# Dilated attention beside a projection: six-step attentions made into one stream of three-unit steps

## The chip, the core and the metric

The kernel runs on one core of a Trainium2 chip. The metric is the device time of one execution in microseconds, from the median of several runs. Engine names are those of the profile: PE is TensorE's matmul, PEld its weight load, DVE is VectorE, ACT is ScalarE, POOL is GpSimd, SP is SyncE, whose queue issues nearly all DMAs here.

## The reference

Two layers on a sequence of 1024 tokens of width 1024, in float32. Layer A is a gated MLP, layer B the attention that the change is about:

```python
for i in range(DEPTH):                       # DEPTH = 2
    h = rms_norm(x, norm_pre[i])
    y = gmlp_mixer(...) if i % 2 == 0 else dilated_attention_mixer(h, b_w_in, b_w_out, cos, sin)
    x = x + rms_norm(y, norm_post[i])

def dilated_attention_mixer(h, w_in, w_out, cos, sin):
    proj = h @ w_in                           # q, k, v of 3 groups x 16 heads x 64, and z
    for g, (window, dilation) in enumerate(((128, 1), (512, 4), (2048, 16))):
        q, k = apply_rope(...), apply_rope(...)
        o, lse = dilated_window_attention(q, k, qkv[:, :, g, 2], window, dilation)
    alpha = softmax(stack(lses), axis=0)      # weights of the three groups
    o = einsum('gbsh,gbshk->bshk', alpha, stack(outs))
    return (o * silu(z)) @ w_out
```

With 1024 tokens each group has eight blocks of 128 queries. A block of group 0 sees its own block and the one before it, in group 1 every second block does, and in group 2 a block sees only itself.

## The kernel before

Everything is written in a tile language whose scheduler sets the order of instructions on DVE, ACT, POOL and SP. The order on PE is that of the code in layer B (a manual schedule).

**The projection stream.** The product of `h` with the weights is cut into chunks: for each quarter `q` of the heads and each group `g` a chunk for V and two for Q and K (one for each pair of heads, `pr`), and now and then one for z. A chunk does seven products in a Strassen scheme, each float32 product as three matmuls on split operands (`mm3`, lines 83 to 85). In the profile these are `p_bv`, `p_bqk` and `p_bz`; below each is called a p. They follow each other without pause, and are the bulk of PE's work from about 790 us to 1825 us. The sums of products (`b_x`, `vt`) are made by ACT and DVE. The Q/K results are rotated on DVE and written to the tiles `Q` and `K` by 16 DMAs of a chunk (lines 703 and 704) on SP's queue.

**Attention between the p's.** `drive()` walks the stream three p's at a time (one yield). At a yield it adds `rate` to a credit, and when the credit is one it takes a step of the first generator in the queue `side`. With `RATE` = 0.16 a step comes every 18 or 21 p's. From chunk (3, 0, 1) on `RATE3` = 0.25 makes it 12. An attention, one of 24, (`attention(q, g, pr)`) becomes ready `WAIT` = 18 yields after its chunk's last product; it treats its eight blocks in four units of two, and has six steps:

```python
for s in range(6):
    if s >= 2: values(s - 2)      # po: V with PT       (line 796)
    if 1 <= s <= 4: transp(s - 1) # pT: St turned       (line 780)
    if s < 4: scores(s)           # s: Q with K         (line 755)
    yield
```

After `scores` DVE subtracts the maximum (line 764, two or four operations of a unit for each head), ACT takes the exponential into `St` (line 767); after `transp` ACT copies the result to `PT` (782); after `values` ACT copies to `oT` (801), and a DMA writes it to `od` (802). `turned()` transposes the V of both pairs (`pvt`, line 675, one step each) as soon as the V chunk is done. Every fourth yield `step_slow()` runs a piece of `merge`, which weighs the three groups' outputs of one pair of heads: it loads `mg`, `mo`, `mw`, multiplies on DVE, and turns the weights on PE (`wT`).

**Buffers.** The tiles `vt`, `Q` and `K` share a ring of five buffers (`qk_tile`). `St` has two buffers, `PT` one, `oT` two of 256 columns, `V` three, `st` (maxima and sums) one. PSUM has two banks for the scores, two for the transposes and one for `po`.

Of the kernel before, what the change touches and what calls it, by code (L numbers as in the profile page):

```python
# [15 lines left out]
P = 128  # L16
T = 1024
D = 1024
# [5 lines left out]
RATE = 0.16  # L24
WAIT = 18
# [3 lines left out]
RATE3 = 0.25  # L29
# [5 lines left out]
def trunk_kernel(  # L35
# [619 lines left out]
    def v_tile(n):  # L655
        return bp.tile([P, D], F32, tag="V", bufs=3, name=n)

    VS, QK, SZ = {}, {}, {}
    YL = {}

    def v_chunk(q, g):
        vts = {}

        def out(th, ct):
            if ct not in vts:
                vts[ct] = qk_tile(f"vt_{q}_{g}_{ct}")
            return vts[ct][:, th * 512:th * 512 + 512]

        def turned():
            for pr in range(2):  # L670
                V = v_tile(f"V_{q}_{g}_{pr}").rearrange("p (b h d) -> p b h d", b=8, h=2)
                for b4 in range(2):
                    pt = psum("t", [P, 4, P], f"pvt_{q}_{g}_{pr}_{b4}")
                    for j in range(4):
                        nc.tensor.transpose(out=pt[:, j, :], in_=toks(vts[pr], g, 4 * b4 + j, 1), identity=ident)
                    nc.scalar.copy(out=V[:, 4 * b4:4 * b4 + 4].rearrange("p j h d -> p j (h d)"), in_=pt)
                VS[q, g, pr] = V
                yield

        return proj_t(wb[q * 10 + g * 3], bops, newb, f"bv{q}{g}", lambda th, ct, o: None, out=out, done=lambda: later(turned(), 4))  # L680

    def qk_chunk(q, g, pr):
# [47 lines left out]
    merged = set()  # L730
    slow = deque()

    def attention(q, g, pr):


        nm = f"{q}_{g}_{pr}"
        Qt, Kt = QK[q, g, pr]
        S, PTs = {}, {}
        st = bp.tile([P, 8, 2, 2], F32, tag="st", bufs=1, name=f"st_{nm}")

        def prev_of(b):
            return (g == 0 and b > 0) or (g == 1 and b % 2 == 1)

        def scores(u):

            pss = [psum("s", [P, 2, 256], f"s_{nm}_{u}_{hh}") for hh in range(2)]
            for j in range(2):
                b = 2 * u + j
                prev = prev_of(b)
                o0 = 0 if prev else P  # L750
                for hh in range(2):
                    hs_ = slice(64 * hh, 64 * hh + 64)
                    q_ = block(Qt[hs_, :], g, b)
                    k_ = block(Kt[hs_, :], g, b, prev)
                    nc.tensor.matmul(out=pss[hh][:, j, o0:256].rearrange("p (n l) -> p n l", l=k_.shape[2]), lhsT=q_, rhs=k_, start=True, stop=True)  # L755
            for j in range(2):
                b = 2 * u + j
                o0 = 0 if prev_of(b) else P
                mk = mask[:, o0:256] if g < 2 else mask2
                St = bp.tile([P, 2, 256], F32, tag="St", bufs=2, name=f"St_{nm}_{u}_{j}")  # L760
                S[u, j] = St
                for hh in range(2):
                    with tc.high_priority(SOON):
                        nc.vector.tensor_tensor_reduce(  # L764
                            out=St[:, hh, o0:256], in0=pss[hh][:, j, o0:256], in1=mk, scale=-0.125, scalar=3.0e38,
                            op0=ALU.add, op1=ALU.min, accum_out=st[:, b, hh, 0:1])
                        nc.scalar.activation(  # L767
                            out=St[:, hh, o0:256], in_=St[:, hh, o0:256], func=AF.Exp, scale=-1.0,
                            bias=st[:, b, hh, 0:1], accum_out=st[:, b, hh, 1:2])

        def transp(u):

            PT = bp.tile([P, 2, 4, P], F32, tag="PT", bufs=1, name=f"PT_{nm}_{u}")
            PTs[u] = PT
            pT = [psum("t", [P, 4, P], f"pT_{nm}_{u}_{hh}") for hh in range(2)]
            use = [2 * j + kk for j in range(2) for kk in range(0 if prev_of(2 * u + j) else 1, 2)]
            sl = slice(1, 4, 2) if g == 2 else slice(use[0], 4)
            for hh in range(2):
                for k in use:
                    nc.tensor.transpose(out=pT[hh][:, k, :], in_=S[u, k // 2][:, hh, k % 2 * P:k % 2 * P + P], identity=ident)  # L780
                with tc.high_priority(SOON):
                    nc.scalar.copy(out=PT[:, hh, sl], in_=pT[hh][:, sl])

        def values(u):

            V, PT, b = VS[q, g, pr], PTs.pop(u), 2 * u
            po = psum("o", [P, 256], f"po_{nm}_{u}")
            if g == 2:
                todo = [(b, 1, 1, 0), (b + 1, 3, 1, P)]
            else:  # L790
                todo = [(b, 1, 2, 0), (b + 1, 3, 1, P)]
                if prev_of(b):
                    todo.insert(0, (b - 1, 0, 1, 0))
            for n, (kb, k, w, o) in enumerate(todo):
                for hh in range(2):
                    nc.tensor.matmul(  # L796
                        out=po[64 * hh:64 * hh + 64, o:o + w * P], lhsT=V[:, kb, hh, :], rhs=PT[:, hh, k:k + w, :].rearrange("p k i -> p (k i)"),
                        start=n == 0, stop=n == len(todo) - 1, skip_group_check=True)
# [3 lines left out]
            nc.sync.dma_start(out=od[q][pr][g][:, u * 256:u * 256 + 256], in_=oT)  # L802

        for s in range(6):
            if s >= 2:
                values(s - 2)
            if 1 <= s <= 4:
                transp(s - 1)
            if s < 4:
                scores(s)  # L810
            if s == 3:
                sv, ws = st.rearrange("p b h s -> p b (h s)"), slice(4 * g, 4 * g + 4)
                if g == 0:
                    nc.sync.dma_start(out=sd[q][pr].rearrange("(b i) w -> i b w", i=P)[:, :, ws], in_=sv)
                elif g == 1:
                    for n in range(2):
                        nc.sync.dma_start(
                            out=sd[q][pr].rearrange("(n i r) w -> n i r w", i=P, r=4)[n, :, :, ws],
                            in_=sv.rearrange("p (r n) w -> n p r w", n=2)[n])
                else:  # L820
                    nc.sync.dma_start(out=sd[q][pr].rearrange("(i b) w -> i b w", b=8)[:, :, ws], in_=sv)
            yield
        if g == 2 and q < 3:
            slow.append(merge(q, pr))

    def merge(q, pr, last=False):
# [15 lines left out]
        m = bp.tile([P, 8, 2], F32, tag="m", bufs=1, name=f"m_{nm}")  # L842
        e = bp.tile([P, 3, 2, 8], F32, tag="e", bufs=1, name=f"e_{nm}")
        nc.vector.tensor_tensor(out=m, in0=nmx[:, :, 0], in1=nmx[:, :, 1], op=ALU.min)
        nc.vector.tensor_tensor(out=m, in0=m, in1=nmx[:, :, 2], op=ALU.min)
        for g in range(3):
            sub(e[:, g].rearrange("p h b -> p b h"), m, nmx[:, :, g])
        nc.scalar.activation(out=e, in_=e, func=AF.Exp)
        for g in range(3):
            mul(sm[:, :, g], sm[:, :, g], e[:, g].rearrange("p h b -> p b h"))  # L850
        add(m, sm[:, :, 0], sm[:, :, 1])
        add(m, m, sm[:, :, 2])
        nc.vector.reciprocal(out=m, in_=m)
        for g in range(3):
            mul(e[:, g], e[:, g], m.rearrange("p b h -> p h b"))
# [7 lines left out]
        wT = bp.tile([P, 256], F32, tag="oT", bufs=2, name=f"wTs_{nm}")[0:48, 0:P]  # L863
# [24 lines left out]
        if last:  # L888
            if pr == 0:
                ws_ = [v_tile(f"mw_{nm}_0"), v_tile(f"mw_{nm}_1"), cos_t]  # L890
            else:
                ws_ = [sin_t, bp.tile([P, D], F32, tag="PT", bufs=1, name=f"mw_{nm}_1"), v_tile(f"mw_{nm}_2")]
            for g in range(3):
                for h in range(2):
                    nc.sync.dma_start(out=ws_[g][64 * h:64 * h + 64, :], in_=wd[q][pr][g, h].partition_broadcast(64))
            yield
            for th in range(2):
                ows = []
                for g in range(3):
                    wv_ = ws_[g][:, HALVES[th]].rearrange("p (i r) -> p i r", r=RUNS[g])  # L900
                    ov = os_[g].rearrange("p (r n i) -> p n r i", n=2, r=RUNS[g])[:, th] if g else os_[0][:, HALVES[th]].unsqueeze(1)
                    mul(wv_, ov.rearrange("p r i -> p i r"), wv_)
                    ows.append(ws_[g][:, HALVES[th]])
# [21 lines left out]
    credit, rate = [0.0], [RATE]  # L925
    now = [0]

    def later(gen, wait=0):
        side.append((now[0] + wait, gen))

    def step_side(force=False):
        while side:
            at, gen = side[0]
            if at > now[0] and not force:
                return False
            try:
                next(gen)
                return True
            except StopIteration:
                side.popleft()  # L940
        return False
# [66 lines left out]
    def fill():  # L1008
# [6 lines left out]
        for gen in busy:  # L1015
            run(gen)
# [7 lines left out]
    def attend():  # L1024
        m = merge(3, 0, True)
        for n, gen in enumerate(busy):
# [111 lines left out]
```

## Time and profile before

| | |
|---|---|
| median of three runs | 1942.67 us (1941.22 to 1943.18) |
| profiled execution | 1939.93 us, span 1938.2 us |
| mean granted PE clock | 0.989 |
| PE busy | 1860.0 us, 96% of the span |
| DVE, ACT, POOL busy | 67%, 52%, 26% |
| DMA | 125 GB/s on average |

PE is busy nearly all of the time, so the question for each instruction is whether it makes PE start its next matmul later, or takes PE's time itself. The times of the trace are microseconds from the start of the span.

### The profile page before, as it was taken

What the parts mean: (1) busy time and instruction counts of PE and PEld (TensorE: products, weight loads), DVE (VectorE), ACT (ScalarE), POOL (GpSimd) and SP (SyncE); (2) the same over time, 40 slices, a digit from 0 to 9 for tenths busy, and PEclk for the clock granted to TensorE, in tenths of its full rate; (3) what the DMA queues carried; (4) which work ended last, traced back from release to release, by engine and by line L of the source; (5) the groups of instructions that cost most, each with busy time, mean ns of one, the idle gap of its engine ahead of it and who ended that gap; (6) DMA issues with size and microseconds to landing.
All of it is one profiled execution on the core that took longest, in us unless ns stands there. A gap on an engine that the chain in (4) does not pass through costs nothing. (4 is left out here: it accounts for less than half of the span.)

```text
span 1938.2 us, 29972 instructions
## 1 busy us (share of the span) xinstructions
PE 1860.0 (96%) x10024; PEld 1492.9 (77%) x10024; DVE 1300.9 (67%) x2518; ACT 1016.1 (52%) x2332; POOL 499.9 (26%) x371
## 2 busy tenths in 40 slices
PE   6899999999999897999999999999999999999898
PEld 6899788888888676877777777777677776777677
DVE  7755866676455886658568783867665776867473
ACT  7544455555544564455545458455465446454831
POOL 4431334334200204212122222222123221122310
PEclk9999999999999998999999999999999999999999
DMA  5332434433267584223244543335542434433863
GB/s 207 99 119 90 140 113 138 122 105 106 77 202 232 173 256 135 81 74 89 72 94 108 158 112 108 79 75 148 147 110 83 99 93 138 123 77 80 228 200 111
DMA packets 233993, 242.25 MB, mean 125 GB/s; under 512 B 98672, under 2 KB 154608, under 8 KB 233840
## 3 DMA queue, kind: packets, MB, share of 16 engines
q1 hardware_dynamic: 233840, 240.34, 43.0%
q8 instruction: 80, 1.31, 0.3%
q14 instruction: 73, 0.60, 0.1%
HBM read 170.46 MB, written 44.63 MB: 111 GB/s over the span
## 5 line engine op out<-in xcount | busy, mean ns | idle before, releaser
L83 PE MATMUL p_bqk<-b_hi,whi_bqk 128*128 128x512 f32 x672 | 274.3, 408 | 1.2 <-DVE b_x_bqk L88 0.9
L85 PE MATMUL p_bqk<-b_hi,wlo_bqk 128*128 128x512 f32 x672 | 263.8, 393 | 0.0
L84 PE MATMUL p_bqk<-b_lo,whi_bqk 128*128 128x512 f32 x672 | 263.2, 392 | 0.0
L767 ACT ACTIVATE St<-St,st 128x128 f32<-128x128 f32 (+1 forms) x384 | 169.2, 443 | 173.6 <-DVE st L764 165.5
L83 PEld LDWEIGHTS p_bqk<-b_hi,whi_bqk 128*128 128x128 f32 x672 | 126.9, 189 | 40.4 <-issue 11.2
L85 PEld LDWEIGHTS p_bqk<-b_hi,wlo_bqk 128*128 128x128 f32 x672 | 126.7, 189 | 28.0
L84 PEld LDWEIGHTS p_bqk<-b_lo,whi_bqk 128*128 128x128 f32 x672 | 127.2, 189 | 23.6
L764 DVE CUSTOM_DVE_ANT_0 St<-s,mask 128x128 f32<-128x128 f32 (+1 forms) x384 | 111.7, 347 | 49.4 <-PE s L755 45.9
L83 PE MATMUL p_bv<-b_hi,whi_bv 128*128 128x512 f32 x336 | 137.6, 410 | 3.0 <-DVE vt L88 1.8
L85 PE MATMUL p_v<-whi_v,a_lo 128*128 128x256 f32 x448 | 128.3, 287 | 4.1 <-DVE sqa L368 2.3
L85 PE MATMUL p_bv<-b_hi,wlo_bv 128*128 128x512 f32 x336 | 131.6, 392 | 0.0
L84 PE MATMUL p_v<-wlo_v,a_hi 128*128 128x256 f32 x448 | 128.2, 287 | 3.5 <-DVE wlo_v L91 3.5
L84 PE MATMUL p_bv<-b_lo,whi_bv 128*128 128x512 f32 x336 | 131.4, 391 | 0.0
L83 PE MATMUL p_v<-whi_v,a_hi 128*128 128x256 f32 x448 | 128.3, 287 | 1.4 <-DVE v_s_v L88 0.8
L91 DVE TENSOR_TENSOR wlo_bqk<-wb_bqk,whi_bqk 128x512 fp32r<-128x512 f32 x96 | 81.4, 848 | 66.7 <-ACT whi_bqk L97 66.7
L91 POOL TENSOR_TENSOR wt_bqk<-wb_bqk,wt_bqk 128x512 f32<-128x512 f32 x48 | 71.7, 1494 | 202.4 <-DMA wb_bqk<-in_wb_dram 110.2
L85 PE MATMUL po<-oh,yl 128*128 128x512 f32 x256 | 100.6, 398 | 3.9 <-DVE yl L91 3.9
L84 PE MATMUL po<-ol,yh 128*128 128x512 f32 x256 | 100.6, 395 | 1.2 <-DVE ol L91 1.2
L83 PE MATMUL po<-oh,yh 128*128 128x512 f32 x256 | 101.3, 397 | 0.2 <-ACT yh L97 0.2
L97 ACT CAST whi_bqk<-wb_bqk 128x512 fp32r<-128x512 f32 x96 | 59.7, 622 | 71.5 <-PE p_bqk L84 44.1
L780 PE MATMUL pT<-ident,St 128*128 128x128 f32 x560 | 88.3, 285 | 7.9 <-ACT St L767 6.7
L91 POOL TENSOR_TENSOR wt_bqk<-wb_bqk,wb_bqk 128x512 f32<-128x512 f32 x24 | 32.8, 1365 | 234.8 <-DMA wb_bqk<-in_wb_dram 190.5
(260 smaller groups left out, 4854.0 us busy)
## 6 DMA issues: line engine op xcount, KB each, us to landing
wb_bqk<-in_wb_dram SPq DMA_DIRECT2D x96, 256.0 KB, 3.5
wr<-in_woa_dram SPq DMA_DIRECT2D x80, 256.0 KB, 3.5
yr<-yad SPq DMA_DIRECT2D x48, 256.0 KB, 3.3
wb_bv<-in_wb_dram SPq DMA_DIRECT2D x48, 256.0 KB, 3.2
Q<-b_c SPq DMA_DIRECT2D x192, 64.0 KB, 2.1
K<-b_c SPq DMA_DIRECT2D x192, 64.0 KB, 2.0
od<-oT SPq DMA_DIRECT2D x96, 128.0 KB, 2.6
mo<-od SPq DMA_DIRECT2D x36, 256.0 KB, 3.4
```

Source lines behind the costliest of these rows:

```text
L83: nc.tensor.matmul(out=pso, lhsT=l_hi, rhs=r_hi, start=start, stop=False, skip_group_check=chained)
L84: nc.tensor.matmul(out=pso, lhsT=l_hi, rhs=r_lo, start=False, stop=False, skip_group_check=chained)
L85: nc.tensor.matmul(out=pso, lhsT=l_lo, rhs=r_hi, start=False, stop=stop, skip_group_check=chained)
L91: (eng or nc.vector).tensor_tensor(out=out, in0=a, in1=b, op=ALU.subtract)
L97: nc.scalar.copy(out=hi, in_=src)
L764: nc.vector.tensor_tensor_reduce(out=St[:, hh, o0:256], in0=pss[hh][:, j, o0:256], in1=mk, scale=-0.125, scalar=3.0e38, op0=ALU.add, op1=A ...
L767: nc.scalar.activation(out=St[:, hh, o0:256], in_=St[:, hh, o0:256], func=AF.Exp, scale=-1.0, bias=st[:, b, hh, 0:1], accum_out=st[:, b, h ...
L780: nc.tensor.transpose(out=pT[hh][:, k, :], in_=S[u, k // 2][:, hh, k % 2 * P:k % 2 * P + P], identity=ident)
```

## The change

The six-step generators are replaced by objects `Unit`. A queue of units runs through all attentions; `attend(unit)` does one step with three units in a row: the transposes of the last unit, the values of the one before it, and the scores of the new one. A unit of groups 0 and 1 has two blocks as before, one of group 2 has four. The V of the second pair of heads is turned after the first two units of the first pair's attention. The rates are lower, the wait shorter, and buffers are dealt out anew: `V` 2, `st` 2, `PT` 2, `oT` one of 512 columns, `St` a tile for each head. The end is rewritten to fit (`ending`), and the last merge uses other tiles.

```diff
-RATE = 0.16
-WAIT = 18
+RATE = 0.125
+WAIT = 16
...
-RATE3 = 0.25
+RATE3 = 0.16
...
-        return bp.tile([P, D], F32, tag="V", bufs=3, name=n)
+        return bp.tile([P, D], F32, tag="V", bufs=2, name=n)
...
+        def done():
+            TURN[q, g] = turned(1)
+            later(turned(0), 4)
...
-            later(attention(q, g, pr), WAIT)
-            if (q, g, pr) == (3, 0, 1):
+            later(lambda: attention(q, g, pr), WAIT)
+            if (q, g, pr) == (3, 2, 1):
                 rate[0] = RATE3
...
+        def __init__(self, att, u):
+            self.q, self.g, self.pr, self.st = att
+            self.n = 4 if self.g == 2 else 2
+            self.b, self.last = self.n * u, self.n * u + self.n == 8
...
+            self.S = [bp.tile([P, 512], F32, tag="St", bufs=2, name=f"St_{self.nm}_{hh}") for hh in range(2)]
...
-            PT = bp.tile([P, 2, 4, P], F32, tag="PT", bufs=1, name=f"PT_{nm}_{u}")
+            self.PT = bp.tile([P, 2, 4, P], F32, tag="PT", bufs=2, name=f"PT_{self.nm}")
...
-            oT = bp.tile([P, 256], F32, tag="oT", bufs=2, name=f"oT_{nm}_{u}")
+            oT = bp.tile([P, 512], F32, tag="oT", bufs=1, name=f"oT_{self.nm}")[:, 0:w]
...
+    def attention(q, g, pr):
+        st = bp.tile([P, 8, 2, 2], F32, tag="st", bufs=2, name=f"st_{q}_{g}_{pr}")
+        units = [Unit((q, g, pr, st), u) for u in range(2 if g == 2 else 4)]
+
+        return units[:2] + [TURN.pop((q, g))] + units[2:] if pr == 0 else units
+
+    going = [None, None]
+
+    def attend(unit):
+
+        if going[0]:
+            going[0].transp()
+        if going[1]:
+            going[1].values()
+        if unit:
+            unit.scores()
+        going[:] = [unit, going[0]]
...
-    credit, rate = [0.0], [RATE]
+    credit, rate = [0.5], [RATE]
```

In the whole program the attentions now break into the p stream 114 times and not 175: 78 steps of transposes, values and scores, four partial ones, 24 of V and 8 of `wT`. The matmuls are the same in number. The copies to `PT` go from 192 to 160, those to `oT`, and their DMAs, from 96 to 80.

Two places show how instructions move; names are tile_q_g_pr_unit, and a row ends with the shape of the result. The first is PE in attention (1, 2, 0), third group. Before, a middle step stands thus between two p's:

```order
L85 MATMUL p10_bv20_12369<-b_hi2_5165,wlo2_bv20_12229 128x512
L796 MATMUL po_1_2_0_0_12373<-PT_1_2_0_0_12305,V_1_2_0_12044 64x128 x4
L780 MATMUL pT_1_2_0_1_0_12382<-ident_69,St_1_2_0_1_0_12320 128x128
L780 MATMUL pT_1_2_0_1_0_12382<-ident_69,St_1_2_0_1_1_12325 128x128
L780 MATMUL pT_1_2_0_1_1_12383<-ident_69,St_1_2_0_1_0_12320 128x128
L780 MATMUL pT_1_2_0_1_1_12383<-ident_69,St_1_2_0_1_1_12325 128x128
L755 MATMUL s_1_2_0_2_0_12390<-K_1_2_0_12062,Q_1_2_0_12061 128x128
L755 MATMUL s_1_2_0_2_1_12391<-K_1_2_0_12062,Q_1_2_0_12061 128x128
```

The matching step of the changed kernel, of which the last p ahead and the first scores are shown (eight rows of scores follow each other, then a p):

```order
L85 MATMUL p00_bqk2_0_0_12400<-b_hi1_5163,wlo1_bqk2_0_0_12341 128x512
L799 MATMUL pT_1_2_0_1_0_12415<-ident_69,St_1_2_0_1_0_12229 128x128 x4
L799 MATMUL pT_1_2_0_1_1_12416<-ident_69,St_1_2_0_1_1_12230 128x128 x4
L815 MATMUL po_1_2_0_0_12427<-PT_1_2_0_0_12198,V_1_2_0_11866 64x128 x8
L766 MATMUL s_1_2_1_0_0_12439<-K_1_2_1_12253,Q_1_2_1_12252 128x128
L766 MATMUL s_1_2_1_0_1_12440<-K_1_2_1_12253,Q_1_2_1_12252 128x128
```

The values now stand between transposes and scores, and a step holds twice as many of each. The second place is PE at the end of the scores of attention (0, 1, 0), before:

```order
L755 MATMUL s_0_1_0_3_0_8960<-K_0_1_0_8512,Q_0_1_0_8511 128x128
L755 MATMUL s_0_1_0_3_1_8961<-K_0_1_0_8512,Q_0_1_0_8511 128x128
L755 MATMUL s_0_1_0_3_0_8960<-K_0_1_0_8512,Q_0_1_0_8511 128x256
L755 MATMUL s_0_1_0_3_1_8961<-K_0_1_0_8512,Q_0_1_0_8511 128x256
L83 MATMUL p00_bv02_8709<-b_hi7_5175,whi7_bv02_8818 128x512
L84 MATMUL p00_bv02_8709<-b_lo7_5176,whi7_bv02_8818 128x512
```

And after, where `p20` is a partial product of V chunk (0, 2), one of its seven:

```order
L799 MATMUL pT_0_1_0_2_0_8990<-ident_69,St_0_1_0_2_0_8940 128x128 x3
L799 MATMUL pT_0_1_0_2_1_8991<-ident_69,St_0_1_0_2_1_8941 128x128 x3
L815 MATMUL po_0_1_0_1_9000<-PT_0_1_0_1_8915,V_0_1_0_8584 64x256 x2
L815 MATMUL po_0_1_0_1_9000<-PT_0_1_0_1_8915,V_0_1_0_8584 64x128 x2
L766 MATMUL s_0_1_0_3_0_9008<-K_0_1_0_8512,Q_0_1_0_8511 128x128
L766 MATMUL s_0_1_0_3_1_9009<-K_0_1_0_8512,Q_0_1_0_8511 128x128
L766 MATMUL s_0_1_0_3_0_9008<-K_0_1_0_8512,Q_0_1_0_8511 128x256
L766 MATMUL s_0_1_0_3_1_9009<-K_0_1_0_8512,Q_0_1_0_8511 128x256
L83 MATMUL p20_bv02_8886<-b_hi3_5167,whi3_bv02_8899 128x512
L84 MATMUL p20_bv02_8886<-b_lo3_5168,whi3_bv02_8899 128x512
L85 MATMUL p20_bv02_8886<-b_hi3_5167,wlo3_bv02_8900 128x512
```

On DVE the changed kernel has, right behind the four reductions of this unit's scores, the two sums into `vt`, of which the first reads `p20` before the p's shown may add to it; the `ISA` rows are the reductions of line 774 and the reads of their results:

```order
L774 ISA St_0_1_0_3_0_9014,st_0_1_0_8676<-s_0_1_0_3_0_9008,mask_7392 128x128
L774 ISA st_0_1_0_8676 128x1
L774 ISA St_0_1_0_3_0_9014,st_0_1_0_8676<-s_0_1_0_3_0_9008,mask_7392 128x256
L774 ISA st_0_1_0_8676 128x1
L774 ISA St_0_1_0_3_1_9015,st_0_1_0_8676<-s_0_1_0_3_1_9009,mask_7392 128x128
L774 ISA st_0_1_0_8676 128x1
L774 ISA St_0_1_0_3_1_9015,st_0_1_0_8676<-s_0_1_0_3_1_9009,mask_7392 128x256
L774 ISA st_0_1_0_8676 128x1
L88 TENSOR_TENSOR vt_0_2_1_8952<-p20_bv02_8886,b_x2_0_bv02_8950 128x512
L88 TENSOR_TENSOR vt_0_2_1_8952<-p20_bv02_8886,b_x1_0_bv02_8848 128x512
```

`vt_0_2_1` takes over the ring buffer of this attention's `Q`, so its first sum can't stand ahead of the last scores. Before, 33 p's and another attention step lay between those scores and the p of `p20` that waits for the sum; now there is none.

## Rows read from the trace of the kernel before

**Rows 1.** Page, part 1: busy us (share of the span) and instructions, by engine

```profile
PE 1860.0 (96%) x10024; PEld 1492.9 (77%) x10024; DVE 1300.9 (67%) x2518; ACT 1016.1 (52%) x2332; POOL 499.9 (26%) x371
```

**Rows 2.** PE's waits, 790 to 1665 us: total us, times, longest

```profile
PE pT L780 <- ACT St L767: 5.8, 7, 2.1
PE po L796 <- ACT oT L801: 3.5, 3, 1.7
PE p_bv L83 <- DVE vt L88: 1.8, 1, 1.8
```

**Rows 3.** PE's waits, 1665 to 1825 us

```profile
PE s L755 <- issue: 2.4, 3, 2.0
```

**Rows 4.** Windows: length, busy us of each engine, PE clock, DMA share, GB/s

```profile
790.00:1665.00 875.00, 861.98 (x4746) 659.61 (x4745) 605.62 (x1345) 471.85 (x1293) 202.74 (x136) 1.00 0.41 106
1665.00:1686.00 21.00, 17.58 (x76) 13.57 (x75) 20.47 (x23) 4.49 (x8) 5.89 (x4) 0.96 0.42 108
1686.00:1691.00 5.00, 5.00 (x15) 3.48 (x12) 4.07 (x12) 1.73 (x8) 0.02 (x1) 0.50 0.23 78
...
1765.00:1825.00 60.00, 56.58 (x327) 41.30 (x326) 35.15 (x101) 42.15 (x119) 18.47 (x11) 1.00 0.64 163
```

**Rows 5.** Timeline of PE, scores alone: start, us, line, operation, count

```profile
981.93 0.39 PE L84 MATMUL p_bqk<-b_lo,whi_bqk 128*128 128x512 f32 x1
982.16 0.39 PE L85 MATMUL p_bqk<-b_hi,wlo_bqk 128*128 128x512 f32 x1
982.48 0.71 PE L755 MATMUL s<-K,Q 64*128 64x128 f32 x8
...
983.46 0.39 PE L84 MATMUL p_bqk<-b_lo,whi_bqk 128*128 128x512 f32 x1
```

**Rows 6.** Timeline of PE, a full step of group 2

```profile
1292.07 0.39 PE L85 MATMUL p_bqk<-b_hi,wlo_bqk 128*128 128x512 f32 x1
1292.39 0.66 PE L796 MATMUL po<-PT,V 128*64 128x128 f32 x8
1292.98 0.66 PE L780 MATMUL pT<-ident,St 128*128 128x128 f32 x4
1293.57 0.71 PE L755 MATMUL s<-K,Q 64*128 64x128 f32 x8
...
1294.55 0.39 PE L84 MATMUL p_bqk<-b_lo,whi_bqk 128*128 128x512 f32 x1
```

**Rows 7.** Timeline of PE, eight transposes of V

```profile
1050.51 0.39 PE L85 MATMUL p_bv<-b_hi,wlo_bv 128*128 128x512 f32 x1
1050.75 1.03 PE L675 MATMUL pvt<-ident,vt 128*128 128x128 f32 x8
...
1051.85 0.40 PE L84 MATMUL p_bv<-b_lo,whi_bv 128*128 128x512 f32 x1
```

**Rows 8.** DVE, timeline 1087 us, and reductions by form: busy us, mean ns

```profile
1087.10 0.68 DVE L88 TENSOR_TENSOR vt<-p_bv,b_x_bv 128x512 f32<-128x512 f32 x1
L764 DVE CUSTOM_DVE_ANT_0 St<-s,mask 128x256 f32<-128x256 f32 x176 | 68.3, 419 | 10.6 <-PE s L755 10.6
```

**Rows 9.** PE and SP, timeline, last product of chunk (2, 2, 0) and last K

```profile
1502.31 0.39 PE L85 MATMUL p_bqk<-b_hi,wlo_bqk 128*128 128x512 f32 x1
1514.35 0.61 SPq L704 DMA_DIRECT2D K<-b_c  x1
```

**Rows 10.** Page, part 6: queue, count, KB of one, us to landing

```profile
K<-b_c SPq DMA_DIRECT2D x192, 64.0 KB, 2.0
od<-oT SPq DMA_DIRECT2D x96, 128.0 KB, 2.6
```

**Rows 11.** ACT's waits ahead of line 801, and one of them in its timeline

```profile
1625.70 0.37 ACT L801 COPY oT<-po 128x256 f32<-128x256 f32 x1 [2.29 <-DMA od<-oT]
ACT oT L801 <- DMA od<-oT: 10.8, 4, 3.5
```

More of the change, by code (lines that the diff above doesn't have):

```diff
@@ L728, in z_chunk, with prev, scores @@
         return proj_t(wb[q * 10 + 9], bops, newb, f"bz{q}", z_out, hooks={2: lambda: prep(0), 7: lambda: prep(1)} if q == 3 else None)
-    merged = set()
+    merged, through = set(), set()
     slow = deque()
[L733 to L750, printed above, removed]
+    class Unit:
+        def __init__(self, att, u):
+            self.q, self.g, self.pr, self.st = att
+            self.n = 4 if self.g == 2 else 2
+            self.b, self.last = self.n * u, self.n * u + self.n == 8
+            self.nm = f"{self.q}_{self.g}_{self.pr}_{u}"
+            self.lone = self.g == 2
+            if self.lone:
+                self.use = [[j] for j in range(4)]
+            else:
+                self.use = [[2 * j + kk for kk in range(0 if self.prev(self.b + j) else 1, 2)] for j in range(2)]
+            self.first = self.use[0][0]
+        def prev(self, b):
+            return (self.g == 0 and b > 0) or (self.g == 1 and b % 2 == 1)
+        def scores(self):
+            Qt, Kt = QK[self.q, self.g, self.pr]
+            pss = [psum("s", [P, 512], f"s_{self.nm}_{hh}") for hh in range(2)]
+            for j, use in enumerate(self.use):
+                b, cs = self.b + j, slice(use[0] * P, use[-1] * P + P)
@@ L781, in transp @@
                 with tc.high_priority(SOON):
[L782 to L789, printed above, removed]
-            else:
[L791 to L794, printed above, removed]
+                    nc.scalar.copy(out=self.PT[:, hh, self.first:], in_=pT[hh][:, self.first:])
@@ L795, in values @@
+        def values(self):
+            V, w = VS[self.q, self.g, self.pr], self.n * P
+            po = psum("o", [P, w], f"po_{self.nm}")
+            if self.lone:
+                todo = [(self.b + j, j, 1, j * P) for j in range(4)]
+            else:
+                todo = [(self.b, 1, 2, 0), (self.b + 1, 3, 1, P)]
+                if self.first == 0:
+                    todo.insert(0, (self.b - 1, 0, 1, 0))
+            for n, (kb, k, m, o) in enumerate(todo):
                 for hh in range(2):
@@ L924, in trunk_kernel, with later @@
     side = deque()
-    credit, rate = [0.0], [RATE]
+    credit, rate = [0.5], [RATE]
     now = [0]
-    def later(gen, wait=0):
-        side.append((now[0] + wait, gen))
+    def later(work, wait=0):
+        side.append((now[0] + wait, work))
     def step_side(force=False):
         while side:
-            at, gen = side[0]
+            at, work = side[0]
             if at > now[0] and not force:
                 return False
+            if isinstance(work, Unit):
+                side.popleft()
+                attend(work)
+                return True
+            if callable(work):
+                side.popleft()
+                side.extendleft((at, w) for w in reversed(work()))
+                continue
             try:
-                next(gen)
+                next(work)
                 return True
@@ L940, in step_side @@
                 side.popleft()
+        if (force or rate[0] != RATE) and any(going):
+            attend(None)
+            return True
         return False
@@ L1014, in fill @@
                 yield
-        for gen in busy:
-            run(gen)
+        while step_side(True):
+            pass
         for c in (6, 7):
@@ L1022, in fill, with ending @@
                 yield
-    def attend():
+    def ending():
         m = merge(3, 0, True)
-        for n, gen in enumerate(busy):
-            for _ in gen:
-                if n == len(busy) - 1:
-                    next(m, None)
-                yield
+        while step_side(True):
+            if (3, 2, 0) in through:
+                next(m, None)
+            yield
         yield from m
         yield from merge(3, 1, True)
-    busy = [gen for _, gen in side]
-    side.clear()
-    rest = attend()
+    rest = ending()
     for n, _ in enumerate(fill()):
```

149 lines of the change are left out of this document (73 added, 76 removed).

## The prediction

> **What bounds the kernel.** I read the page first: PE is busy 1860.0 us, 96% [rows 1]. The change touches layer B alone, so windows come next. From 790 to 1665 us PE is busy 861.98 of 875 us at full clock, and DVE and ACT have 605.62 and 471.85 [rows 4]: PE's own work is the bound there, with 13.0 us lost. From 1665 to 1686 us 3.4 us are lost, behind that five microseconds run at clock 0.50 (2.5 us lost), and from 1765 to 1825 us 3.4 us are lost, all by the same rows. That makes 22.3 us. The reader is to see two things to win: these 22 us, and PE's work itself. PE's waits name the first: transposes for the exponentials (5.8 us in 7 waits), values for the copy to `oT` (3.5 in 3), a p of V for the sum into `vt` (1.8 in 1) [rows 2], and later scores that wait for K (2.4; longest 2.0) [rows 3]. A change of some microseconds on PE is therefore a change of the whole; idle time of other engines costs nothing.
>
> **What a step costs PE.** Consecutive p's start 0.227 us apart (0.23 in the first two of [rows 5], which are rounded to 0.01). The cost of an interruption is the time from the p ahead to the second p behind, less two such intervals.
> - Scores alone: 983.46 - 982.16 - 0.454 = 0.846 [rows 5].
> - Values, transposes and scores of one unit of group 2: 1294.55 - 1292.07 - 0.454 = 2.026 [rows 6].
> - Eight transposes of V: 1051.85 - 1050.51 - 0.454 = 0.886, or 0.111 each [rows 7].
>
> Transposes use the array as p's do (128*128 in the rows), and take twice what their 128 columns would at 0.227 for 512. Scores and values use it otherwise (64*128 and 128*64), two heads beside each other. Eight such rows are four pairs, so by the transposes' pitch 4 x 0.11 = 0.44. What is left of 0.846 is 0.41 for two borders (p to scores, scores to p), 0.20 each. The full step has four borders (p, values, transposes, scores, p) and 2.026 - 3 x 0.44 = 0.70 left, 0.175 each. So each time PE goes over between unlike uses it loses 0.17 to 0.20 us, and a transposition next to a p loses nothing.
>
> Now count borders. Before, an attention has 2 + 2 + 4 + 4 + 2 + 2 = 16 in its six steps, 24 times: 384. After, a step is transposes, values, scores: p to transposes is free, three borders are left. 78 steps and 8 borders in the partial ones make 242. Two things are in this: the order within a step, and the third group, whose 32 units of each kind have 16 groups where 32 stood. The difference is 142 x 0.175 = **-25 us**. No row shows values directly ahead of scores. From below: if that border cost nothing, 78 more go, -38. From above: if it cost as much as leaving for a p and coming back, two, 78 are added, and 64 x 0.175 = -11. I take one border, because values to transposes and transposes to scores are single borders in [rows 6] and fit the same price.
>
> The Trainium skill bears on this, "TensorEngine Tiling (Array Packing)", section Key Properties under Tiling Modes: going from one tiling mode to another drains TensorE, while other tiles of the same mode don't. By that rule values to scores is one drain like any other, and the term is the -25 above; by a price for the distance between the uses it would be the -11. The trace agrees as far as it goes: four borders of 0.175 and two of 0.20.
>
> **Waits that go.** Steps are now 24 p's apart, 5.4 us and the step itself, where they were 18 (4.1 us), and 18 (16 at the end) instead of 12 in the dense stretch. The distance from scores to their transposes becomes 24, that from transposes to values at least 18, where values stood as few as 12 p's behind their transposes or directly behind the last `oT` copy. I take the waits on `oT` and `wT`, the one on `vt` at 1087 us, and one of the seven long ones on the exponentials as gone: 3.5 + 1.8 + 1.0, with their starts about 7 of the 13.0 us. The other 6 stay: there DVE itself is held by `merge`, which waits for DMAs, and a longer distance gives only 0.3 us more, since before the values (about 1.0 us) stood ahead of the transposes. The scores' wait near 1684 us, with the low clock behind it, was 5.9 us; it goes from this place. The dense stretch, 3.4 us, goes. Sum **-16.3**.
>
> **Waits that come.**
> - `vt`: in four V chunks, (0, 2), (1, 1), (2, 1), (3, 1), a p now follows scores directly and needs a sum that stands on DVE behind four reductions. Two pairs of reductions (one of 0.419 [rows 8]; the shorter ones 0.29) and the sum of 0.68 [rows 8] are 2.1 us after the first scores' end, of which the rest of the scores covers some 0.8: 1.3 each, **+5.2** (bounds +4 and +9, the latter with another DVE operation ahead). Behind the waiting p stands all of PE.
> - Q and K: the last product of chunk (2, 2, 0) starts at 1502.31 and ends 0.39 later; its last K is issued at 1514.35 [rows 9] and lands 2.0 later [rows 10], 13.65 us after. The first scores came 66 p's on and did not wait. With the shorter `WAIT` and the coarser steps they come after 48 p's at (0, 0, 0), (1, 2, 0) and (2, 2, 0): 10.9 us and 1.7 of transposes and values, 12.6 at most. That is 1.1 each, and in four other chunks where other steps lie between, about 1 each: **+7.6** (bounds +3.6 and +12, if each late one also brings a stretch at clock 0.50 as in [rows 4]).
> - `oT`: one buffer, so ACT's copy waits for the DMA of the copy before. Landing takes 2.6 us from issue [rows 10], a step is 8.0 us, so only a DMA held on SP's queue is late. **+2.5**, one such place; above, see the rivals.
>
> Fewer copies on ACT, the smaller `merge`, and `V` with two buffers lie beside PE's stream: DVE and ACT have 269 and 403 us idle in the 875 [rows 4]. Were ACT the bound, 48 copies fewer of 0.37 us [rows 11] would be worth 18 us more. The matmuls of the end are the same, and I take nothing there.
>
> Sum: -25 - 16.3 + 15.3 = **-26.0**, from the profiled 1939.93 to about 1914. The median of the runs was 2.7 us above that execution; I forecast **1915 us**.
>
> **Rivals.**
> 1. *Values to scores cost two borders.* For it: the two uses differ in both sides of the array. Against: nothing in the rows charges a border by what lies on its two sides. Then -11 instead of -25: 1929 us.
> 2. *The new waits don't come*, since the whole stream shifts and with it what DMAs and DVE meet: the four `vt` sums find DVE free, Q and K land in time. For it: Q and K had landed at 66 p's without a wait, and their delay is SP's issue time of 0.6 us each, which other orders shorten. Against: the distance 0 of the `vt` sums is fixed by the order. 1915 - 13 = 1902 us.
> 3. *The single `oT` decides, and the kernel is slower.* SP issues in order; the 16 DMAs of Q and K take 0.61 each [rows 9], so a DMA of `oT` behind all of them lands 9.8 + 2.6 = 12.4 us after its copy, against 8.0 until the next copy. ACT then stands 4.4 us, with the exponentials of the new scores queued behind it; the transposes have 1.3 us of slack, so PE loses up to 3.1. Before, two buffers gave twice the time, and still ACT waited 10.8 us in 4 places, in one of them 2.29 with PE behind it [rows 11]. In SP's new order 17 of 80 of these DMAs have 12 or more Q and K issues since the one before. All 17 at full price are 53 us in place of the 2.5: 1965 us. From nine on the gain is gone, from 11 the kernel is slower (1915 - 2.5 + 34 = 1947). Against: 96 copies waited in 4 places [rows 11], so most of these DMAs are issued before such a queue builds up. The Trainium skill, "Trainium Kernel Development and Optimization", section Best Practices, advises two buffers for what is moved by DMA; here the trace shows waits even with two.
> 4. *PE's work is less, but another bound takes it:* weights for the p's, prepared by POOL, ACT and DVE, come late. Against: no wait of a p on weights in [rows 2, 3]. With half of the 25 lost, 1928 us.
>
> **Chances.** Forecast 0.55 (1904 to 1925 for itself), rival 1 0.17, rival 2 0.13, rival 3 0.10, rival 4 0.05. About 0.2%, 3.9 us, is what a measurement can tell from no change. Only rival 3 reaches above 1939, and not in all of its cases; with what the others leave open: faster 0.88, same 0.05, slower 0.07. Range 1898 to 1938: below it lies the free border together with rival 2, above it rival 3 in earnest.
>
> **What would show it.** In the changed profile: a full step of group 2 (eight transposes, sixteen values, sixteen scores) between two p's costing 3 x 0.88 + 3 x 0.18 = 3.2 us; 3.5 would speak for rival 1. PE's busy time falling by some 20 us with the same matmuls. Waits of `p_bv` on `vt` at four places; waits of scores on K or `issue` at the starts of attentions; no waits of `po` on `oT` of more than a few microseconds in sum, and ACT's on `oT` DMAs below about 15. The forecast is wrong if ACT stands for `oT` in nine places or more, or if PE's busy time stays.

## The result and the profile after

| | before | changed |
|---|---|---|
| median | 1941.95 us (1938.92 to 1943.18, 4 runs) | 1913.93 us (1912.29 to 1919.63, 4 runs) |
| ratio, 95% interval | | 0.9863 (0.9839 to 0.9888) |
| profiled execution, span | 1938.2 us | 1913.5 us |

The kernel is 1.4% faster; 1915 us had been forecast. The page of the changed kernel, part 1, to set beside [rows 1]:

```profile
PE 1834.7 (96%) x10024; PEld 1507.0 (79%) x10024; DVE 1310.4 (68%) x2518; ACT 1002.7 (52%) x2280; POOL 503.6 (26%) x371
```

The same 10024 matmuls take PE 25.3 us less, and the span is 24.7 us shorter. Nearly all of it is one stretch. First the window of the kernel before from 790 us to its last values, then that of the changed kernel (length, busy time of each engine, clock, DMA share):

```profile
790.00:1825.00 1035.00, 1015.14 (x5566) 774.22 (x5565) 713.29 (x1581) 560.72 (x1540) 241.76 (x160) 1.00 0.41 107
```

```profile
790.00:1801.00 1011.00, 987.22 (x5563) 786.08 (x5562) 717.54 (x1582) 548.25 (x1487) 246.15 (x160) 0.99 0.42 108
```

Almost the same matmuls lie in both. The stretch is 24.0 us shorter: busy time falls by 27.9 us, idle time rises from 19.9 to 23.8. So the gain is PE's work, and the waits are a little worse. Busy time holds some time at a low clock too: taken in windows of 1 us, PE's busy time times what the clock lacked to 1.00 is an estimated 4.9 us in the stretch before and 6.8 in that of the changed kernel. Without it PE's work fell by some 30 us. A full step of the third group, timeline of PE:

```profile
1267.28 0.39 PE L85 MATMUL p_bqk<-b_hi,wlo_bqk 128*128 128x512 f32 x1
1267.51 1.03 PE L799 MATMUL pT<-ident,St 128*128 128x128 f32 x8
1268.47 1.09 PE L815 MATMUL po<-PT,V 128*64 128x128 f32 x16
1269.50 1.16 PE L766 MATMUL s<-K,Q 64*128 64x128 f32 x16
...
1270.93 0.40 PE L84 MATMUL p_bv<-b_lo,whi_bv 128*128 128x512 f32 x1
```

It costs 1270.93 - 1267.28 - 0.454 = 3.20 us, the 3.2 of the prediction with one border between values and scores (3.5 had stood for two). It does the work of two full steps of before, which cost 2 x 2.03 [rows 6].

PE's waits in the changed kernel, 790 to 1800 us, all five groups over 0.6 us (total, times, longest), beside [rows 2, 3]:

```profile
PE p_bv L83 <- DVE vt L88: 11.1, 4, 3.2
PE s L766 <- DMA K<-b_c: 7.5, 10, 1.4
PE pT L799 <- ACT St L777: 3.1, 7, 0.9
PE p_bqk L83 <- ACT b_x_bqk L240: 0.9, 2, 0.4
PE s L766 <- issue: 0.7, 1, 0.7
```

The values wait for `oT` no more, and the transposes for the exponentials half as long. In their place stand the two waits that the prediction named: four of V's p's for `vt`, and ten of scores for K. The first is twice as long as forecast. How one of them comes about (ACT, DVE and PE, one timeline):

```profile
1081.23 0.37 ACT L820 COPY oT<-po 128x256 f32<-128x256 f32 x1 [3.71 <-DMA od<-oT]
...
1083.13 0.90 DVE L91 TENSOR_TENSOR wlo_bqk<-wt_bqk,whi_bqk 128x512 fp32r<-128x512 f32 x1 [5.77 <-ACT whi_bqk L97]
1084.13 1.58 DVE L91 TENSOR_TENSOR wlo_bqk<-wb_bqk,whi_bqk 128x512 fp32r<-128x512 f32 x1
1085.64 0.68 DVE L91 TENSOR_TENSOR wlo_bqk<-wt_bqk,whi_bqk 128x512 fp32r<-128x512 f32 x1
1086.24 0.41 DVE L774 CUSTOM_DVE_ANT_0 St<-s,mask 128x256 f32<-128x256 f32 x1
...
1087.62 0.68 DVE L88 TENSOR_TENSOR vt<-p_bv,b_x_bv 128x512 f32<-128x512 f32 x1
...
1088.35 0.50 PE L83 MATMUL p_bv<-b_hi,whi_bv 128*128 128x512 f32 x1 [3.18 <-DVE vt L88]
```

ACT stands 3.71 us for the DMA of the copy before, with the casts of weights queued behind it; DVE stands 5.77 us for those casts, then does three splits in a row, then the reductions of scores that had been ready on PE since 1085, then the sum; PE waits 3.18 us. ACT's stop in this is a DMA that left late and then had to land: SP issued it at 1076.90, 2.8 us after the values were done, and ACT stood from 1077.52 to 1081.23. Ahead of the other two long waits ACT stood 3.52 and 3.72 us at the same copy (1344.93 and 1610.71 us), the first of them put down to PE by the profile, though a DMA of `oT` issued at 1340.80 was on its way. About a microsecond after PE goes on, the clock is low. Windows behind three of the four such waits:

```profile
1089.50:1092.00 2.50, 2.50 (x8) 1.97 (x7) 0.00 (x0) 0.00 (x0) 1.02 (x1) 0.52 0.54 95
1352.40:1355.80 3.40, 3.40 (x9) 2.62 (x8) 0.00 (x0) 0.00 (x0) 1.27 (x1) 0.51 0.76 180
1618.70:1621.60 2.90, 2.90 (x8) 2.27 (x7) 0.00 (x0) 0.00 (x0) 1.27 (x1) 0.50 0.67 158
```

A fourth such stretch (1506.0 to 1509.4 us, clock 0.51) stands behind two waits of scores on K, 0.99 and 0.84 us. The kernel before has two between 790 and 1825 us, which begin at 1380.5 and 1684 us.

### The profile page after: what moved, and what is told of

It reads as the page before. It is cut to its first block, busy times and chain, and to the rows that moved or that the text cites. A ratio compares the mean times of both kernels' runs of the same rounds, so it can differ in the third digit from the quotient of the medians.

```text
span 1913.5 us, 29729 instructions
## 1 busy us (share of the span) xinstructions
PE 1834.7 (96%) x10024; PEld 1507.0 (79%) x10024; DVE 1310.4 (68%) x2518; ACT 1002.7 (52%) x2280; POOL 503.6 (26%) x371
## 4 chain that ended last, share of the span: by engine, by line
PE 72%; DVE 10%; DMA 5%; issue 3%; SPq 2%; ACT 2%; POOL 1%; DVEq 0%; POOLq 0%; ACTq 0%
PE p_bqk L83 6%; PE p_bqk L84 6%; PE p_bqk L85 6%; PE p_bv L83 4%; PE p_bv L85 3%; PE p_bv L84 3%; PE s L766 3%; PE po L815 3%; PE p_z L83 3%; PE p_z L84 2%; PE p_z L85 2%; PE pT L799 2%; PE p_u L83 2%; PE p_u L84 2%; PE po L84 2%
## 5 line engine op out<-in xcount | busy, mean ns | idle before, releaser
L83 PE MATMUL p_bqk<-b_hi,whi_bqk 128*128 128x512 f32 x672 | 270.2, 402 | 1.0 <-ACT b_x_bqk L240 0.9
L83 PE MATMUL p_bv<-b_hi,whi_bv 128*128 128x512 f32 x336 | 137.7, 410 | 12.2 <-DVE vt L88 11.1
L766 PE MATMUL s<-K,Q 64*128 64x128 f32 (+1 forms) x768 | 85.8, 342 | 8.5 <-DMA K<-b_c 7.5
```

The costliest lines, as they stand in the source:

```text
L83: nc.tensor.matmul(out=pso, lhsT=l_hi, rhs=r_hi, start=start, stop=False, skip_group_check=chained)
L766: nc.tensor.matmul(out=pss[hh][:, cs].rearrange("p (n l) -> p n l", l=k_.shape[2]), lhsT=q_, rhs=k_, start=True, stop=True)
```

## The experiments

All are edits of the changed kernel, and leave nothing of the reference out. Times are compared by their ratio to the kernel before, run on the same chip; the changed kernel's is 0.9863.

**Values first.** One line order within the step undone:

```diff
-        if going[0]:
-            going[0].transp()
         if going[1]:
             going[1].values()
+        if going[0]:
+            going[0].transp()
```

> The changed kernel with one line order undone: in each step the values stand ahead of the transposes again, so a step is values, transposes, scores. Steps, units, rates and buffers stay. Border theory (each going over between unlike uses of the array costs 0.15 to 0.18 us): 76 steps get a fourth border, PE's busy time rises by 11 to 14 us and the kernel is at 1925 to 1928 us. Rival (the gain came from fewer and wider spaced steps alone, the order within a step is free): 1911 to 1917 us. The transposes come about 1 us later, which can save up to 3 us of their waits on the exponentials under either.

Measured: 1925.78 us, ratio 0.9920 (0.9896 to 0.9943), 12 us above the changed kernel. The page's first line:

```profile
PE 1848.3 (96%) x10024; PEld 1505.0 (78%) x10024; DVE 1303.9 (68%) x2518; ACT 1011.2 (53%) x2280; POOL 501.9 (26%) x371
```

and the window up to the last values:

```profile
790.00:1811.00 1021.00, 1001.90 (x5583) 785.01 (x5582) 715.91 (x1584) 557.19 (x1489) 247.06 (x161) 0.99 0.41 107
```

PE's busy time rises by 13.6 us with the same matmuls, while idle time in the window falls from 23.8 to 19.1. One more stretch at the low clock is in it (935.0 to 938.8 us at 0.56, where the changed kernel has none), an estimated 1.7 us. Some 12 us are left for the order, 0.16 for each of some 76 steps. A full step of the third group, timeline of PE:

```profile
1277.09 0.39 PE L85 MATMUL p_bqk<-b_hi,wlo_bqk 128*128 128x512 f32 x1
1277.41 1.09 PE L815 MATMUL po<-PT,V 128*64 128x128 f32 x16
1278.43 1.09 PE L799 MATMUL pT<-ident,St 128*128 128x128 f32 x8
1279.45 1.16 PE L766 MATMUL s<-K,Q 64*128 64x128 f32 x16
...
1280.88 0.40 PE L84 MATMUL p_bv<-b_lo,whi_bv 128*128 128x512 f32 x1
```

It costs 1280.88 - 1277.09 - 0.454 = 3.34 us, 0.14 more than in the changed kernel, for the same matmuls and one border more. The order within the step alone is worth nearly half of the change's gain, and it is work of PE, not a wait.

**Small units.** The third group in units of two blocks:

```diff
-            self.n = 4 if self.g == 2 else 2
+            self.n = 2
...
-        units = [Unit((q, g, pr, st), u) for u in range(2 if g == 2 else 4)]
+        units = [Unit((q, g, pr, st), u) for u in range(4)]
...
```

> The changed kernel with units of two blocks in the third group as in the first two, so four steps of an attention there and not two: 16 more steps, each of half the matmuls. Border theory: 16 x 3 borders of 0.175 are 8.4 us more on PE, 1921 to 1924 us. Rival (what made the third group cheaper was the longer time between its steps): the waits decide, PE's busy time without them is as before, and the time moves by under 3 us.

Measured: 1937.07 us, ratio 0.9992 (0.9978 to 1.0005): all of the gain is lost, 23 us by the times and 25 by the ratios, where 8 had been expected. PE is busy 1847.8 us, 13.1 more than in the changed kernel. A step of the third group costs 1.88 us here, about as three borders and three times 0.44 make it, so the 16 steps' borders are their 8 us. The other part neither theory had. The 16 steps more, at 24 p's each, fill the rest of the stream: the last values end at 1833 us, with the last p, where the changed kernel has them at 1801, 13 us before it. But that by itself cost nothing that the traces show, for behind the last p both kernels need the same time (windows of this one and of the changed kernel):

```profile
1832.90:1933.20 100.30, 87.98 (x385) 71.68 (x385) 59.04 (x111) 25.52 (x60) 14.98 (x16) 0.96 0.56 179
```

```profile
1813.70:1913.50 99.80, 88.59 (x383) 71.62 (x381) 60.08 (x103) 25.22 (x59) 16.46 (x16) 0.96 0.51 159
```

The loss lies ahead of it: between 790 us and the last p PE is busy 14.0 us more (1012.55 against 998.54) and idle 5.2 us more. Of the busy time an estimated 3 us are low clock, in six stretches where the changed kernel has four. One of them follows a wait of a p of z near the end (timeline and window):

```profile
1796.37 0.79 PE L83 MATMUL p_bz<-b_hi,whi_bz 128*128 128x512 f32 x1 [2.22 <-ACT b_x_bz L240]
```

```profile
1793.50:1799.50 6.00, 3.78 (x10) 2.67 (x9) 2.02 (x10) 5.29 (x14) 0.68 (x1) 0.72 0.19 19
```

So borders and low clock make up some 11 us of the 19.7 that lie between the two profiled executions, idle time ahead of the last p 5; the rest was not taken apart.

**Closer steps.** The old rate, and the old dense stretch, each alone:

```diff
-RATE = 0.125
+RATE = 0.16
```

> The changed kernel with the old rate of steps, 0.16 in place of 0.125: a step every 18 or 21 p's, units and order as in the change. Theory that the wider spacing took waits away: PE's waits of transposes on the exponentials rise from 3.1 to 7 to 10 us, ACT's waits on the oT DMAs from 10 to over 15, and the time is 1917 to 1922 us. Rival (spacing is worth little, since the waits stand where DVE or SP are held by other work): 1911 to 1916 us, with the waits of scores on K changing by at most 3 us either way, as their places shift.

```diff
-RATE3 = 0.16
+RATE3 = 0.25
...
-            if (q, g, pr) == (3, 2, 1):
+            if (q, g, pr) == (3, 0, 1):
```

> The changed kernel with the old dense stretch: rate 0.25 (12 p's between steps) from chunk (3, 0, 1) on, in place of 0.16 from (3, 2, 1). If closer steps cost waits, as the 3.4 us did that the prediction booked for that stretch: 3 to 5 us more waits after 1690 us, 1916 to 1919 us in all. Rival (the fourth quarter's attentions are held back by their Q and K, and steps come no earlier): within 1.5 us of the changed kernel.

Measured: 1929.25 us, ratio 0.9947 (0.9932 to 0.9961), and 1935.13 us, ratio 0.9976 (0.9964 to 0.9988): 15 and 21 us worse, far more than either theory said. PE's waits at the old rate, from 790 to 1830 us:

```profile
PE s L766 <- DMA K<-b_c: 11.4, 14, 3.2
PE pT L799 <- ACT St L777: 6.8, 10, 2.4
PE po L815 <- ACT oT L820: 6.1, 3, 2.8
```

The three waits of a step on what the step before should have finished all grow (from 7.5, 3.1 and none), and ACT's waits for the DMAs of `oT` from 11.9 to 14.3; the waits on `vt` are gone, since other p's follow the scores. In the dense one the values wait 4.9 us in 2 places, and ACT 17.2 us in 8. At closer steps the single `oT` buffer reaches PE: the values wait 6.1 and 4.9 us for its copy. Neither edit is clean, though. The program sends off the last units of an attention early once `rate[0] != RATE`: with equal rates that never holds, and with the early switch it holds too soon, so part of both losses can be that. The spacing's own share stays open.

**Two `oT` buffers** of 256 columns, the same memory:

```diff
-            oT = bp.tile([P, 512], F32, tag="oT", bufs=1, name=f"oT_{self.nm}")[:, 0:w]
+            for o in range(0, w, 256):
+                oT = bp.tile([P, 256], F32, tag="oT", bufs=2, name=f"oT_{self.nm}_{o}")
```

> The changed kernel with two oT buffers of 256 columns in place of one of 512, the same memory; a unit of four blocks is copied and sent in two halves, 16 more copies and DMAs. Theory that the single buffer is behind a good part of the late sums into vt: ACT's waits on these DMAs (11.9 us in 4 places) go to under 3, PE's waits on vt from 11.1 to 6 to 8, and the time falls by 4 to 7 us to about 1908. Rival (vt is late by its place on DVE alone): PE's waits on vt stay at 10 to 12 and the time at 1912 to 1916 us.

Measured: 1915.99 us, ratio 0.9876 (0.9854 to 0.9898), no gain. Up to 1800 us ACT waits 9.9 us in 3 places, where the changed kernel has 9.6 in 3 (11.9 in 4 up to 1830), and PE 11.4 us on `vt`. At the place shown above two DMAs of `oT` now leave SP together, behind a store of `merge` and a load of weights (SP's queue in this kernel):

```profile
1079.31 0.33 SPq L950 DMA_DIRECT2D ybd<-mo  x1
1079.73 0.38 SPq L171 DMA_DIRECT2D wb_bqk<-in_wb_dram  x1
1080.21 0.88 SPq L822 DMA_DIRECT2D od<-oT  x2
```

and ACT waits 3.28 us there. Both buffers had filled while SP stood, and both DMAs left late. The number of buffers is not what makes ACT stop here; that it is SP's queue is borne out below, where K's DMAs, or those of `oT`, leave it.

**The sum aside.** The first sum of V's second half stays in its operand's buffer, and ACT copies it to `vt`:

```diff
-                c = self.out(1, 1) or x2
-                self.each(add, c, self.pc, x2)
+                self.each(add, x2, self.pc, x2)
+                c = self.out(1, 1) or x2
+                if c is not x2:
+                    self.each(lambda o, a: nc.scalar.copy(out=o, in_=a), c, x2)
```

> The changed kernel, but the first sum of a V chunk's second half is made in its own operand buffer and copied by ACT into vt, so that the p's of the product that follows wait for no free ring buffer. Twelve more copies on ACT of about 0.6 us. Theory that these sums cost PE their whole wait and the slow clock behind it: waits of p_bv on vt (11.1 us in 4 places) go, the stretches at half clock behind them too (1.2 to 1.6 us lost in each of three), and the time falls by 9 to 15 us, to 1900 to 1905. Rival (the wait stands for a DVE and ACT that are late anyway, and PE meets them at the next scores or transposes): the waits on K and on the exponentials rise by as much, 1910 to 1916 us.

Measured: 1910.28 us, ratio 0.9842 (0.9820 to 0.9864), some 3.6 us better than the changed kernel, with intervals that overlap. PE's waits, and the window that had been at clock 0.52:

```profile
PE pT L801 <- ACT St L779: 6.8, 12, 1.6
PE s L768 <- DMA K<-b_c: 6.6, 9, 1.2
```

```profile
1089.50:1092.00 2.50, 2.50 (x12) 2.04 (x12) 1.06 (x8) 1.82 (x8) 0.44 (x1) 1.00 0.40 119
```

The wait on `vt` is gone as a whole, and so is the low clock there; but transposes now wait 3.7 us more, and 3 us of what the stretch gains (it ends 7.5 us earlier) are given back behind it, 116 us against 113 from the last values to the end. Between the two theories, nearer the rival.

**K from POOL's queue**, alone and with the sum aside:

```diff
+                eng = nc.sync if i < 2 else nc.gpsimd
-                nc.sync.dma_start(out=half_of(dst[o:o + 32, :], g, th), in_=by_block(xc[32 * i:32 * i + 32, :], g))
+                eng.dma_start(out=half_of(dst[o:o + 32, :], g, th), in_=by_block(xc[32 * i:32 * i + 32, :], g))
```

> The changed kernel with the eight DMAs of K issued from POOL's queue in place of SP's. Theory that Q and K are late at the first scores by SP's 0.6 us for each of 16 issues: PE's waits of scores on K (7.5 us in 10) go below 3, DMAs of oT come earlier and ACT waits less than 6 us for them, and the time falls by 5 to 8 us to about 1907. Rival (POOL issues more slowly than SP, or stands for the rotated K in front of the sums of weights that it makes): waits on K stay or grow, p's wait for weights, 1914 us or more.

> The sum aside and K from POOL's queue, both in one kernel. If the two waits are separate, their gains add: 1910 less 5 to 7, some 1903 to 1905 us. If they are the same time lost under two names, or the sums of merge take their place on DVE, 1908 to 1911 us.

Measured: 1928.23 us, ratio 0.9948 (0.9935 to 0.9960), and 1924.87 us, ratio 0.9941 (0.9918 to 0.9963). The rival held: scores wait 16.6 us on K, in 4 places, where they had waited 7.5. POOL's timeline ahead of one of the two longest waits of scores on K (6.9 us, ending at 1247.6 us):

```profile
1236.36 0.58 POOL L708 DMA_DIRECT2D K<-b_c  x1
1236.95 2.42 POOL L91 TENSOR_TENSOR wt_bv<-wb_bv,wt_bv 128x512 f32<-128x512 f32 x1
1239.33 1.72 POOL L91 TENSOR_TENSOR wb_bv<-wb_bv,wb_bv 128x512 f32<-128x512 f32 x1
1241.00 1.71 POOL L91 TENSOR_TENSOR wt_bv<-wb_bv,wt_bv 128x512 f32<-128x512 f32 x1
1242.65 0.59 POOL L707 DMA_DIRECT2D K<-b_c  x1
```

Three sums of weights, 5.9 us, stand between two issues. But SP is free of half of its Q and K, and there ACT waits for `oT` only 1.0 us, once, and PE on `vt` 8.4 us in 4, none over 2.2. So of the 11.1 us on `vt` 2.7 came through ACT's stop, and 2.1 each is the price of the place. Small units show the same 8.4 us.

**The `oT` DMAs from ACT's queue**, alone and with the sum aside:

```diff
-            nc.sync.dma_start(out=od[self.q][self.pr][self.g][:, self.b * P:self.b * P + w], in_=oT)
+            nc.scalar.dma_start(out=od[self.q][self.pr][self.g][:, self.b * P:self.b * P + w], in_=oT)
```

> The changed kernel with the 80 DMAs of oT issued from ACT's queue, right behind the copies, in place of SP's. Two buffers had not taken ACT's waits away, since the DMAs themselves stood on SP behind those of Q, K and merge. Theory that SP's queue is what delays them, and that ACT's stop makes the splits of weights, the reductions and with them the sums into vt late: ACT's waits on oT (11.9 us) go below 2, PE's waits on vt from 11.1 to 6 or 7, and the time falls by 4 to 8 us to 1906 to 1910. Rival (vt waits for three DVE operations that stand ahead of the reductions whatever ACT does): waits on vt at 9 or more, 1911 to 1915 us; the issues themselves may cost ACT up to 0.6 us each, in its idle time.

> The sum aside and the oT DMAs from ACT's queue. If the sums and ACT's stops are separate losses, the gains add: 1910 less 3 to 5, about 1906 us. If the sum aside had already hidden ACT's stops: 1909 to 1911 us.

Measured: 1923.19 us, ratio 0.9920 (0.9903 to 0.9936), and 1919.74 us, ratio 0.9897 (0.9881 to 0.9913), 9 us worse than without in both. In the first of them the profile puts 17.8 us of ACT's waits down to these DMAs, in two rows:

```profile
ACT St L777 <- DMA od<-oT: 11.2, 4, 3.4
...
ACT oT L820 <- DMA od<-oT: 6.6, 2, 4.0
```

But the first row names the wrong releaser: each of its four exponentials starts 0.11 to 0.12 us after DVE has read the maximum that it needs. One of them (DVE and ACT, timeline):

```profile
1142.50 0.28 DVE L774 CUSTOM_DVE_ANT_0 St<-s,mask 128x128 f32<-128x128 f32 x1
1142.71 0.08 DVE L774 DVE_READ_ACCUMULATOR2_ANT st<- 128x1 f32 x1
...
1142.83 0.40 ACT L777 ACTIVATE St<-St,st 128x128 f32<-128x128 f32 x1 [3.40 <-DMA od<-oT]
```

The exponential at the same place of the changed kernel waits 4.09 us, put down to DVE. So ACT stands for `oT` only in the second row, at 1804 and 1811 us. In the rest of the stream its stops are gone, and the sums into `vt` wait 8.4 us as with K on POOL's queue, between the 6 or 7 of the theory and the 9 of the rival. The theory holds in its mechanism, SP's queue and ACT's stop, and fails in the time: PE's waits on the exponentials go to 7.4 us and on K to 10.3. Why these two grow was not found out.

**Later first scores.** With the sum aside, the third group's attention of the first pair of heads in each quarter, and the very first attention of all, become ready four yields later, so that their scores come a step later:

```diff
-            later(lambda: attention(q, g, pr), WAIT)
+            later(lambda: attention(q, g, pr), WAIT + (4 if pr == 0 and (g == 2 or q + g == 0) else 0))
```

> The sum aside, and the first attention of a pair in the third group, and the very first one, become ready 20 yields after their chunk and not 16, so that their first scores stand a step (24 p's) further from the last product of Q and K. Theory that these scores come too early (6.6 us of waits on K, 2.3 to 2.7 at each of the third group's): the waits there go, 4 to 6 us, to 1904 to 1907 us. Rival (the stream is one step later, and what it meets is as late, or steps pile up at the end): 1908 us or more.

> The sum aside, the oT DMAs from ACT's queue and the later first scores of the third group together. If all three act apart: 1900 to 1903 us; if they share the same lost time, no better than the best of the others, 1905 to 1909 us.

Measured: 1901.14 us, ratio 0.9798 (0.9782 to 0.9814), and, with the DMAs on ACT's queue too, 1908.09 us, ratio 0.9834 (0.9816 to 0.9852). The first of them is the best of all, 39 us below the kernel before on the same chip and 0.7% below the changed one, with intervals apart. PE's waits in it:

```profile
PE pT L801 <- ACT St L779: 6.0, 11, 1.4
PE s L768 <- DMA K<-b_c: 2.9, 5, 1.0
```

The waits on K fall from 6.6 to 2.9, and 9 us are gained over the sum aside alone where 4 to 6 were expected. Some 3 us of the rest are clock: the sum aside still has two stretches at half clock, and with later scores there is none up to the last values (two windows of the sum aside, then one of this kernel):

```profile
1106.90:1110.40 3.50, 3.50 (x18) 1.97 (x17) 2.47 (x4) 2.78 (x7) 0.00 (x0) 0.51 0.65 192
1236.90:1240.30 3.40, 3.40 (x10) 2.60 (x9) 2.91 (x18) 1.93 (x10) 0.00 (x0) 0.53 0.25 96
```

```profile
790.00:1789.00 999.00, 986.79 (x5576) 782.34 (x5575) 720.01 (x1583) 555.03 (x1501) 248.34 (x161) 1.00 0.43 110
```

The first of the two stands behind a wait of 1.58 us on the exponentials, the second behind two waits of scores, 0.72 and 0.88 us. The later scores without the sum aside were not run.

## Why the prediction was right

- **Borders, -25 us.** Right in kind. PE's busy time fell by 27.9 us in the stretch (25.3 in all), and by some 30 without the time at the low clock, so the term is about 5 us too small; where these lie was not found out. The border between values and scores, of which no row of before told, costs what the others do: the step came out at 3.20 us. The first experiment shows the cause by itself: the same matmuls with one border more in each of some 76 steps are some 12 us more of PE's time, 0.16 each, and 0.14 in the step shown. The first rival (two borders) falls.
- **Waits that go, -16.3, and waits that come, +15.3.** The sum, -1.0, came out as idle time 3.9 us up and some 2 us more at the low clock, 7 us on the wrong side of the forecast. The `vt` sums were booked with +5.2 (bounds 4 and 9) and are 11.1, with a low clock behind each of three: the step that was off is the cover of 0.8 us, which there is not (2.1 each remain when ACT doesn't stop), and that DVE might first have three splits to do, late by ACT's stop. Q and K were booked with 7.6, though 3 x 1.1 and 4 x 1 are 7.3, and are 8.2 (7.5 and 0.7). Against that, waits on the exponentials fell to 3.1, where about 6 us had been left standing. The 875 us of before were called full clock, and hold one stretch at half clock (1380.5 to 1384 us).
- **The sum is in part luck.** A border term 5 us too small and a wait term 7 us too good nearly cancel: -26.0 was forecast, and the spans differ by 24.7 us.
- **The single `oT`.** Booked with 2.5. Values never wait for it; ACT does in 4 places, and 2.7 us of that reach PE through `vt`. The third rival did not decide. Its premise, that SP's queue holds these DMAs, is what was found; that two buffers would help against it is not. At closer steps the one buffer does cost values up to 6.1 us.
- **The second rival** (the new waits don't come) falls for `vt`, whose place is fixed, and for K in this kernel. The last experiment shows that K's waits hang on where the steps stand. The fourth (late weights) falls too: no wait of a p on weights is among the five groups above.

What the prediction left out is how the parts hang together. The wider spacing goes with larger units that make fewer steps: with small units at that spacing the steps fill the stream to its end, and the whole gain is gone, only part of it by borders. What the spacing alone is worth was not shown.

## What to carry to other kernels

Where PE is the bound, count how often it changes between matmuls of unlike shape in the array, not only how long the matmuls are: the price of one change can be read from two rows with different numbers of them, and an order with fewer changes is worth trying by itself, since it moves no work. Before a wait for a buffer is met by another buffer, look at what its release stands behind: here the DMA queue was in order, and a second buffer filled while the queue stood. When the profile puts a wait down to an instruction that has nothing to do with the waiting one, look at what else ended just before: here the "DMA" of four exponentials was DVE.

## What the runs showed of the hardware

- Each change between unlike matmuls costs TensorE 0.14 to 0.20 us here; transposes beside full-width matmuls cost next to nothing more (eight of them cost PE 0.886 us [rows 7], and a run of eight is 0.43 us longer than one of four, 1.03 against 0.60, which is 0.86 for eight).
- After waits of PE of some 3 us the granted clock fell to about 0.5, the lower of its two levels, about a microsecond after PE had gone on, though PE was busy all through; without the wait the same place ran at 1.00. Shorter waits had it in one run and not in another: behind a wait of 1.9 us for the first sum into `vt` the clock stayed at 1.00 in the changed kernel (930 to 934 us) and was 0.56 with values first (935.0 to 938.8).
- A DMA moved to another engine's queue is held by that engine's own work: K on POOL stood behind 5.9 us of sums. `oT` on ACT's queue took away ACT's stops ahead of the sums, and the kernel was 9 us slower even so.
